# A two-layer encoder trunk: the memory's keys and values become the first chunk of work, and the start is laid out anew around them

## The chip, the cores and the metric

The kernel runs on one core of a Trainium2 chip. The metric is the device time of one execution in microseconds; where it is run several times, the median counts.

## What is computed

A trunk of two layers over 512 tokens of width 1024, with 256 memory tokens beside it. Layer 0 mixes tokens by dilated window attention with three windows, layer 1 by grouped-query attention; both also attend to the memory with four heads. Cut to what matters:

```python
for i in range(DEPTH):
    h = rmsnorm(x, norm_g[i])
    mem_h = rmsnorm(mem, mem_norm_g[i])
    ...
        proj = jnp.einsum('bsd,de->bse', h, w_in_a[j])
    ...
    kv = jnp.einsum('bnd,de->bne', mem_h, w_kv).reshape(Bn, N, 2, MEM_HEADS, HEAD_DIM)
    k = rmsnorm(kv[:, :, 0], kn_g)
    v = kv[:, :, 1]
    ...
    y = jnp.concatenate([o_mix, o_mem], axis=-1) * jax.nn.silu(gate)
    x = x + jnp.einsum('bse,ed->bsd', y, w_out[i])
```

The memory's keys and values of a layer depend on `mem`, a norm row and `w_mem_kv` alone, so they can be made at any time before the memory attention of that layer.

## The kernel before, in words

Every projection is done in float32 by three matmuls in a reduced format: each operand is split into a high part (a cast on ScalarE, ACT) and a remainder (a subtraction on VectorE, DVE). `mm3` (L162) issues the three. A weight piece of 128x1024 goes through three steps: a load of 512 KB (`W.dma`, L224), the cast into `wh` (L285) and the remainder into `wo` (L295). `wh` and `wo` have four buffers each (`RING`), so the cast of a piece waits until TensorE (PE) has read the piece four places before.

The list `PLAN` names the chunks of the program. There are two kinds. `s_chunk` (L352) is one level of Strassen's scheme: seven products in place of eight, and for these VectorE or POOL's transfers also make sums of weight quarters (T1 on VectorE at L251, T2, T3 and T4 by accumulating transfers; in the very first chunk T2 too on VectorE, L259) and VectorE makes sums of the activations. `chunk` (L331), reached through `proj_t` (L485), is a plain product without sums. Before, the order at the start is: the value product of the first attention group (`s_chunk(512, H, ev_v0, pre=second)`, 14 groups of 12 matmuls), the memory's keys and values (`mem_kv(0, ...)`, L593, two chunks of four groups), then the memory queries (`s_chunk(256, H, ev_qm)`), whose matmuls are 256 columns wide.

Each engine runs its own list in order. The order is set by the order of the Python calls and by a small driver that counts groups as slots: `spawn(gen, delay)` lets a generator do a step every so many slots. `prep()` makes the rest of the normed and transposed x, `setup()` the gain products and, on POOL, the rotary tables (L878), `mem_norm(0)` loads and norms the memory.

The norm of a token block is three functions: `norm_1` (L450) makes sums of squares on ScalarE (or half on VectorE) and the inverse root on POOL, `norm_2` (L463) multiplies on VectorE by the root and by the norm row, `norm_3`/`put_h`/`turn4` (L467) transpose four 128x128 blocks on TensorE and split them on ScalarE and VectorE. The norm row is needed on all 128 partitions: `row_bank` (L557) makes it by a product with a row of ones in TensorE, which leaves it in PSUM; `row_load` (L551) loads it 128 times over, 512 KB.

Results of products lie in four PSUM banks (`pj`, L146) that are given out in turn. A bank is free when its last reader is done. The keys are read out of their bank twice: by the sums of squares on ScalarE (L529) and by `head_mul` on VectorE (L534). The values are read by L608 on ScalarE and L610 on VectorE.

Of the kernel before, what the change touches and what calls it, by code (L numbers as in the profile page):

```python
# [21 lines left out]
TCKW = {}  # L22
NBIG, NM4, NS2, SCRATCH = 7, 23, 13, 2048
RING, LEAD = 4, 2
XW, BOTH = (1, 2, 0, 5), False
BULK, ACTIVE, MEM_AT, SET_AT, WARM, MEM_B, PREP_Y, ACC_AT, PREP_B, HALF, SET_B = 2, 2, 5, 15, 1, 12, 1, 4, 1, {"a": 3, "b": 3, "o": 0}, 11
MEM_STEP = 1, 1
MEM_D = 4
PD, W_EARLY = 1, True
EO = 1, 2, 2, 1, 1  # L30
YB = {"m": (2, 2), "k": (1, 1, 1), 0: (1, 2, 1), 1: (1, 2, 1)}
Y = [3, 2, 2, 2, 3, 2, 2, 1, 1, 1]
# [1 line left out]
A_ORDER = "01234567mab"  # L34

PLAN = ["W2"] + ["T2"] * 2 + ["W1", "W2s"] + ["W2" if c.isdigit() else "W1" for c in A_ORDER[1:]] + ["W2"] + ["O1"] * 2 + ["T2b"] * 2 + ["W1b"] * 7 + ["W2b"] + ["O1"] * 2
T1_DMA = 17
KEEP = {"T2": 6, "T2b": 4, "O1": 4, "W1": 9, "W2": 10, "W2s": 9, "W1b": 7, "W2b": 9}


class Driver:
# [83 lines left out]
def trunk_kernel(ctx: ExitStack, tc: tile.TileContext, x, mem, wall, norm_g, mem_norm_g, gcol,  # L125
# [48 lines left out]
    LOADS = (("21", "21"), ("11", "11"), ("T1", "12"), ("T2", "22"), ("22", "22"), ("T3", "12"))  # L174
    GROUPS = {"T2": (2, 2), "T2b": (2, 2), "O1": (1, 4)}

    class Weights:
        def __init__(self):
            self.items, self.last, self.need, self.allocs, self.sums = [], [], [], [], []
            self.users = {}  # L180
            d = g = 0
            for c, kind in enumerate(PLAN):
                base = len(self.items)
                if kind in GROUPS:
                    units, nb = GROUPS[kind]
                    for u in range(units):
                        for x in (2 * u, 2 * u + 1):
                            self.items.append((c, "P", x))
                            self.last.append(g + (u + 1) * nb - 1)
                            self.allocs.append(((c, "P", x), d, kind))  # L190
                            self.users[c, "P", x] = 1
                            d += 1
                        self.need += [base + 2 * u + 2] * nb
                    g += units * nb
                else:
                    n = 1 if kind in ("W1", "W1b") else 2
                    at = {k: d + i * n for i, k in enumerate(("21", "11", "12", "22"))}
                    d += 4 * n
# [11 lines left out]
            assert d == wall.shape[0], (d, wall.shape)  # L210
# [27 lines left out]
        def sum(self, force=False, want=None):  # L238

            for n, (key, d) in enumerate(self.sums[:8]):  # L240
# [3 lines left out]
                if k == "T1" and c >= T1_DMA:  # L244
                    if not self.ripe(self.load_at, key, force):
                        continue
                    G.dma_start(self.tile[key], wall[d], accum_op=ALU.add)
                elif k == "T1":
                    if not (self.ripe(self.load_at, key, force) and self.ripe(self.at, (c, "11", x), force)):
                        continue  # L250
                    V.tensor_tensor(self.tile[key], self.tile[key], self.tile[c, "11", x], ALU.add)  # L251
                    self.use((c, "11", x))
                elif k == "T2":
                    if not (self.ripe(self.load_at, key, force) and self.ripe(self.at, (c, "T1", x), force, 1 if c < T1_DMA else None)):
                        continue
                    if c:
                        G.dma_start(self.tile[key], self.tile[c, "T1", x], accum_op=ALU.add)
                    else:
                        V.tensor_tensor(self.tile[key], self.tile[key], self.tile[c, "T1", x], ALU.add)  # L259
# [15 lines left out]

        def hi(self, force=False):
            i = self.n_hi
            if i >= len(self.items) or not self.ripe(self.at, self.items[i], force, 1 if self.items[i][1] == "T1" and self.items[i][0] < T1_DMA or self.items[i][:2] == (0, "T2") else None):
# [49 lines left out]

    W = Weights()

    def chunk(units, nb, group, evac):  # L331

        ps = [None] * nb
        for u in range(units):
# [3 lines left out]
            for b in range(nb):  # L338
                if u == 0:
                    ps[b] = pj()  # L340
                group(w, u, b, ps[b])
                drv.free()
                W.advance()
# [138 lines left out]

    NAT = [nat(b) for b in range(4)]

    def proj_t(act, sels, evac):  # L485
# [5 lines left out]
        chunk(2, len(sels), group, evac)  # L491

    part = {}

# [59 lines left out]
        nc.sync.dma_start(t, src.to_broadcast([128, D]))  # L554
        rows[name] = halves(t)

    def row_bank(name, times=1):  # L557

        r = [at("row") for _ in range(2)]
        for j in (1, 0):  # L560
            for _ in range(times):
                T.matmul(r[j], ones, rows[name][j][0:1, :], start=True, stop=True)
# [30 lines left out]
    def mem_kv(layer, M):  # L593
# [18 lines left out]
        proj_t(M, NAT[:2], ev_k)  # L612
        proj_t(M, NAT[:2], ev_v)
        return kt_, vt_

# [220 lines left out]
    xv = x.rearrange("(p c) d -> c p d", c=4)  # L836
    xt = [m4(name="x") for _ in range(4)]
    rows = {}
    nc.scalar.dma_start(ident, ident_d)
    row0 = m4(name="row0")[0:1, :]  # L840
    nc.sync.dma_start(row0, norm_g[0:1, :])
    rows["x0"] = halves(row0)
    for c, n in enumerate(XW):
        nc.sync.dma_start(xt[c], xv[c])
        W.dma(n)
# [3 lines left out]
    nc.sync.dma_start(mask, mask_d)  # L849
    nc.sync.dma_start(tabA, tab_a.rearrange("p (b c d) -> p b c d", b=2, c=4))  # L850
    nc.sync.dma_start(grA[:, 0:3], qn_a[0:1, :, 0:32].to_broadcast([128, 3, 32]))
    nc.sync.dma_start(grA[:, 3:6], kn_a[0:1, :, 0:32].to_broadcast([128, 3, 32]))
    H, H2 = {}, {}
    xb = [halves(t) for t in xt]
    nst = {}

    def prep():

        s1, sums = [], []
        for c in range(2):  # L860
            norm_2(xb[2 + c], nst[2 + c], first)
            s1.append(sum_h(xb[2 + c]))
            yield 1
        for c in range(2):
            sums_h(H, xb[c], xb[2 + c], c, s1[c], sums)
# [2 lines left out]

    def setup():

        V.tensor_tensor(gk, gc[:, 0:3], gc[:, 3:6], ALU.mult)
        V.tensor_scalar(gk, gk, QS, None, ALU.mult)
        V.tensor_scalar(gc[:, 6:8], gc[:, 6:8], QS, None, ALU.mult)
# [5 lines left out]
                            grA[:, None].to_broadcast([128, 4, 6, 32]), ALU.mult)  # L879
            yield 1  # L880

    first = row_bank("x0", WARM)

    def busy(n):

        T.matmul(at("busy")[:, 0:n], ones, rows["x0"][0][0:1, 0:n], start=True, stop=True)

    busy(512)
    nst[0] = norm_1(xb[0], True)
    W.hi(True)  # L890
    norm_2(xb[0], nst[0], first, (1,))

    def mid():
        busy(128)
        W.lo()
        nst[1] = norm_1(xb[1], BOTH)

    put_h(H, "12", 0, xb[0][1], mid, True)
    if W_EARLY:
        W.hi(True)  # L900
    norm_2(xb[1], nst[1], first, (1,))
    norm_2(xb[0], nst[0], first, (0,))
    norm_2(xb[1], nst[1], first, (0,))

    def second():

        put_h(H, "12", 1, xb[1][1])
        if not W_EARLY:
            W.hi(True)
        put_h(H, "11", 0, xb[0][0])  # L910
        nst[2] = norm_1(xb[2], BOTH)
        W.lo()
        put_h(H, "11", 1, xb[1][0])
        W.hi(True)
        nst[3] = norm_1(xb[3], BOTH)

    drv.spawn(prep(), PD)
    drv.spawn(setup(), SET_AT)
# [7 lines left out]
        nc.sync.dma_start(v0w[2 * i + u][:, j * 512:(j + 1) * 512], t)  # L926
        yield 1

    drv.spawn(mem_norm(0), MEM_AT)
    s_chunk(512, H, ev_v0, pre=second)  # L930
    km, vm = mem_kv(0, Ms[0])

    od = dram.tile([12, 128, S], F32, name="od", bufs=1)
    o_done = set()
# [581 lines left out]
```

## Time and profile before

| | |
|---|---|
| median of three runs | 978.88 us (977.35 to 979.84) |
| the profiled execution | 977.34 us, its span 975.5 us |
| PE, DVE, ACT, POOL busy | 97%, 81%, 69%, 35% of the span |
| granted TensorE clock | 1.00 throughout |
| first real matmul | 10.11 us |
| first matmul of the memory queries | 86.81 us |

A profile row of the timeline reads: start, duration, engine, line of the kernel, operation, what it writes and reads, shape, and in brackets how long its engine had been idle and which instruction ended that. In the table of waits the columns are: who waited for whom, sum, number of times, the longest. `pj` is a bank of a product, `wh` and `wo` are the two parts of a weight piece, `xT` is a bank of transposes, `h`, `hS` and `act` are transposed activations, `sn` is a result taken out of its bank.

### The profile page before, as it was taken

The numbers are of one execution on the slowest core, as the hardware profiler recorded it, in microseconds if no ns is written. First come the engines' busy times: TensorE is split into PE (matmuls) and PEld (weight loads), VectorE is DVE, ScalarE is ACT, GpSimd is POOL, SyncE is SP. The second block draws the span as 40 slices with busy tenths as digits, with TensorE's granted clock in tenths as the row PEclk, the third lists the DMA queues.
The fourth block names the chain that finished last, engine by engine and source line by source line (L and its number), as shares of the span: only waits on it lengthen the run. The fifth ranks groups of instructions, "written<-read, shape, count | busy, mean of one in ns | idle before, by whom it ended". The sixth has DMA issues, their size and how long they took to land.

```text
span 975.5 us, 16658 instructions
## 1 busy us (share of the span) xinstructions
PE 949.6 (97%) x5728; PEld 836.1 (86%) x5728; DVE 791.0 (81%) x1409; ACT 675.0 (69%) x1687; POOL 343.6 (35%) x484
## 2 busy tenths in 40 slices
PE   8899999999999999999999998998999999999998
PEld 5689888888888888888899996887999999998776
DVE  6997776888888888888888999768788997769863
ACT  5555689686868686868685756555588887878760
POOL 1122423556454545454635011314443231011001
PEclk9999999999999999999999999999999999999999
DMA  8979846969686868785959898879695696877644
GB/s 340 312 261 339 221 103 175 291 122 265 144 262 145 262 147 260 152 257 131 282 129 275 244 202 252 255 259 350 168 215 139 177 242 167 219 194 176 180 140 130
DMA packets 88982, 209.27 MB, mean 215 GB/s; under 512 B 25281, under 2 KB 36033, under 8 KB 88898
## 3 DMA queue, kind: packets, MB, share of 16 engines
q1 hardware_dynamic: 70034, 146.28, 43.4%
q0 software_dynamic: 17568, 59.78, 32.6%
q10 hardware_dynamic: 1296, 2.16, 0.6%
q8 instruction: 45, 0.74, 0.3%
q14 instruction: 39, 0.32, 0.1%
HBM read 157.79 MB, written 12.65 MB: 175 GB/s over the span
## 4 chain that ended last, share of the span: by engine, by line
PE 82%; DVE 6%; DMA 5%; ACT 3%; POOL 2%; issue 1%; SPq 0%; DVEq 0%; ACTq 0%; POOLq 0%
PE pj L163 21%; PE pj L165 21%; PE pj L164 21%; PE qT L541 2%; DMA og<-od 2%; PE sa L1043 1%; PE oo L1145 1%; DVE wo L295 1%; PE pt L1124 1%; PE sa L1039 1%; PE ptb L1348 1%; DMA odb<-o 1%; PE xT L471 1%; DMA wl<-wl 1%; DMA og<-odb 1%
## 5 line engine op out<-in xcount | busy, mean ns | idle before, releaser
L285 ACT CAST wh<-wl 128x1024 fp32r<-128x1024 f32 x255 | 270.4, 1062 | 82.4 <-PE pj L165 38.4
L295 DVE TENSOR_TENSOR wo<-wl,wh 128x1024 fp32r<-128x1024 f32 x255 | 314.2, 1237 | 11.9 <-ACT wh L285 11.4
L163 PE MATMUL pj<-wh,hS 128*128 128x512 f32 (+1 forms) x448 | 164.3, 367 | 1.8 <-DVE sn L377 1.8
L164 PE MATMUL pj<-wo,hS 128*128 128x512 f32 (+1 forms) x448 | 158.1, 353 | 2.6 <-DVE wo L295 2.4
L165 PE MATMUL pj<-wh,hS 128*128 128x512 f32 (+1 forms) x448 | 158.2, 353 | 0.0
L163 PE MATMUL pj<-wh,h 128*128 128x512 f32 (+1 forms) x336 | 123.4, 367 | 0.4 <-ACT h L157 0.4
L164 PE MATMUL pj<-wo,h 128*128 128x512 f32 (+1 forms) x336 | 118.8, 353 | 2.0 <-DVE wo L295 2.0
L165 PE MATMUL pj<-wh,h 128*128 128x512 f32 (+1 forms) x336 | 118.9, 354 | 0.0
L420 POOL TENSOR_TENSOR rstd<-mse,half 128x4 f32<-128x4 f32 (+2 forms) x98 | 101.8, 1039 | 8.2
L164 PEld LDWEIGHTS pj<-wo,hS 128*128 128x128 f32 x448 | 85.0, 190 | 13.4 <-DVE wo L295 3.5
L165 PEld LDWEIGHTS pj<-wh,hS 128*128 128x128 f32 x448 | 84.7, 189 | 12.4 <-DVE hS L160 0.3
L163 PEld LDWEIGHTS pj<-wh,hS 128*128 128x128 f32 x448 | 84.8, 189 | 11.7 <-DVE sn L377 2.0
L360 ACT COPY sn<-pj 128x512 f32<-128x512 f32 x132 | 73.8, 592 | 15.5 <-PE pj L165 11.8
L419 POOL TENSOR_SCALAR mse<-hss 128x4 f32<-128x4 f32 (+1 forms) x86 | 42.8, 498 | 115.2 <-ACT junk L529 111.3
L529 ACT ACTIVATE junk<-sn 128x128 f32<-128x128 f32 x264 | 79.2, 310 | 0.2 <-DVE sn L371 0.2
L987 POOL TENSOR_TENSOR ta<-sn,tabs 128x128 f32<-128x128 f32 (+1 forms) x64 | 36.9, 579 | 118.8 <-DVE sn L534 90.4
L164 PEld LDWEIGHTS pj<-wo,h 128*128 128x128 f32 x336 | 64.0, 190 | 9.6 <-DVE wo L295 2.3
L165 PEld LDWEIGHTS pj<-wh,h 128*128 128x128 f32 x336 | 63.7, 190 | 9.2 <-DVE h L160 0.2
L163 PEld LDWEIGHTS pj<-wh,h 128*128 128x128 f32 x336 | 63.9, 190 | 7.8 <-ACT h L157 0.7
L377 DVE TENSOR_TENSOR sn<-pj,sn 128x512 f32<-128x512 f32 x99 | 67.5, 683 | 3.3 <-PE pj L165 3.0
L269 POOL DMA_DIRECT2D wl<-wl x33 | 29.2, 886 | 111.3 <-DVE wo L295 58.9
L163 PE MATMUL pj<-hS,wh 128*128 128x256 f32 x192 | 55.9, 291 | 0.0
(229 smaller groups left out, 2465.7 us busy)
## 6 DMA issues: line engine op xcount, KB each, us to landing
wl<-in_wall_dram SPq DMA_DIRECT2D x222, 512.0 KB, 7.0
wl<-wl POOLq DMA_DIRECT2D x64, 512.0 KB, 5.9
wl<-in_wall_dram POOLq DMA_DIRECT2D x42, 512.0 KB, 8.3
acc<-sn POOLq DMA_DIRECT2D x16, 256.0 KB, 5.7
od<-o SPq DMA_DIRECT2D x12, 256.0 KB, 5.2
og<-od SPq DMA_DIRECT2D x12, 256.0 KB, 5.9
odb<-o SPq DMA_DIRECT2D x12, 256.0 KB, 3.6
og<-odb SPq DMA_DIRECT2D x12, 256.0 KB, 3.9
```

Of the source, the lines that this page charges most:

```text
L163: T.matmul(o, lh, rh, start=start, stop=False, skip_group_check=True)
L164: T.matmul(o, lh, rl, start=False, stop=False, skip_group_check=True)
L165: T.matmul(o, ll, rh, start=False, stop=stop, skip_group_check=True)
L269: G.dma_start(self.tile[key], self.tile[c, "T2", x], accum_op=ALU.add)
L285: A.copy(wh, self.tile[self.items[i]])
L295: V.tensor_tensor(wo, self.tile[key], wh.bitcast(F32), ALU.subtract)
L360: A.copy(t, b)
L377: V.tensor_tensor(t, b, t, ALU.subtract if q == "12" else ALU.add)
L419: G.tensor_scalar(e, ss, EPS, None, ALU.add)
L420: G.tensor_tensor(r, e, half[:, 0:n], ALU.pow)
L529: A.activation(jk, p[:, j * 128:(j + 1) * 128], AF.Square, scale=QS, accum_out=ss[:, j:j + 1])
L987: G.tensor_tensor(ta[:, 0:n], xn[:, 0:n, 0:32], ropeA[:, 0, b, s0:s0 + n], ALU.mult)
```

## The change

1. The first chunk is the memory's keys, the second its values, the third the value product of x (`SEQ = [1, 2, 0, ...]`; the layout of the weights in memory stays).
2. SP's queue at the start is: two norm rows, the memory's two blocks with two weight pieces between, two more pieces, then x with weights between. The loads of the mask and of the rotary tables, which followed the first eight weight pieces, are issued by `setup()` in the fifteenth slot, and its other steps follow four slots later.
3. The memory's norm row comes by `row_bank` from one row (before: a load of 512 KB). The layer's norm row comes through `row_bank` too, into two of the `pj` banks, and two copies on ScalarE take it from there to SBUF. The 512-wide `busy` matmul is left out.
4. The memory's first half-blocks are normed and transposed ahead of the first group; the others in `ahead(u, b)`, which the chunk calls right before a group. All four blocks of x are normed in `prep()`.
5. The T2 sum of the value product is made by POOL's transfer, as in the other chunks, and no more by VectorE.

Cut to its core:

```diff
-PD, W_EARLY = 1, True
+PD = 2
...
+SEQ = [1, 2, 0] + list(range(3, len(PLAN)))
 T1_DMA = 17
-KEEP = {"T2": 6, "T2b": 4, "O1": 4, "W1": 9, "W2": 10, "W2s": 9, "W1b": 7, "W2b": 9}
+KEEP = {"T2": 8, "T2b": 4, "O1": 4, "W1": 9, "W2": 10, "W2s": 9, "W1b": 7, "W2b": 9}
...
-                    if c:
-                        G.dma_start(self.tile[key], self.tile[c, "T1", x], accum_op=ALU.add)
-                    else:
-                        V.tensor_tensor(self.tile[key], self.tile[key], self.tile[c, "T1", x], ALU.add)
+                    G.dma_start(self.tile[key], self.tile[c, "T1", x], accum_op=ALU.add)
...
+                if pre:
+                    pre(u, b)
                 group(w, u, b, ps[b])
...
+    row1 = m4(name="row1")[0:1, :]
+    nc.sync.dma_start(row1, norm_g[0:1, :])
+    rows["x0"] = halves(row1)
+    for b in range(2):
+        nc.sync.dma_start(mt[b], mem[b * 128:(b + 1) * 128])
+        W.dma(1)
+    W.dma(2)
...
+    for c in range(4):
+        nc.sync.dma_start(xt[c], xv[c])
+        if c % 2:
+            W.dma(2)
...
     def setup():
 
+        nc.sync.dma_start(mask, mask_d)
+        nc.sync.dma_start(tabA, tab_a.rearrange("p (b c d) -> p b c d", b=2, c=4))
+        nc.sync.dma_start(grA[:, 0:3], qn_a[0:1, :, 0:32].to_broadcast([128, 3, 32]))
+        nc.sync.dma_start(grA[:, 3:6], kn_a[0:1, :, 0:32].to_broadcast([128, 3, 32]))
+        yield 4
...
-    first = row_bank("x0", WARM)
+    first = row_bank("m0", WARM)
+    gain = row_bank("x0", 1, pj)
+    rows["x"] = halves(m4(name="row"))
+    for j in (1, 0):
+        A.copy(rows["x"][j], gain[j])
...
-    busy(512)
-    nst[0] = norm_1(xb[0], True)
+    mb, M = [halves(t) for t in mt], Act(NM)
+    nst = [norm_1(mb[0], True)]
     W.hi(True)
-    norm_2(xb[0], nst[0], first, (1,))
+    norm_2(mb[0], nst[0], first, (0,))
...
+    def ahead(u, b):
+
+        if (u, b) == (0, 1):
+            norm_3(mb[1], M, 128, 0)
+            for c in range(2):
+                norm_2(mb[c], nst[c], first, (1,))
+        if (u, b) == (1, 0):
+            for c in range(2):
+                norm_3(mb[c], M, 128 * c, 1)
...
-    drv.spawn(mem_norm(0), MEM_AT)
-    s_chunk(512, H, ev_v0, pre=second)
-    km, vm = mem_kv(0, Ms[0])
+    km, vm = mem_kv(0, M, ahead)
+    s_chunk(512, H, ev_v0)
```

What stands in the engines' lists at two places follows. First ScalarE's list at the start, before; `x_78` and `x_79` are the first two blocks of x, `wh_130` is the first weight piece:

```order
L434 ACTIVATE warm_76<-half_72 128x1
L839 DMA ident_68<-in_ident_dram 128x128
L458 ACTIVATE sq_119,ss_118<-x_78 128x512
L285 CAST wh_130<-wl_86 128x1024
L458 ACTIVATE sq_144,ss_143<-x_79 128x512
L458 ACTIVATE sq_146,ss_143<-x_79 128x512
L157 CAST h12_134<-xT_135 128x4x128
```

The same place after; `m_82` and `m_83` are the memory's blocks, `row_119` and `row_118` the banks with the layer's norm row:

```order
L438 ACTIVATE warm_76<-half_72 128x1
L844 DMA ident_68<-in_ident_dram 128x128
L906 COPY row_122<-row_119 128x512
L906 COPY row_122<-row_118 128x512
L462 ACTIVATE sq_130,ss_129<-m_82 128x512
L287 CAST wh_141<-wl_90 128x1024
L462 ACTIVATE sq_154,ss_153<-m_83 128x512
L462 ACTIVATE sq_156,ss_153<-m_83 128x512
L158 CAST act_125<-xT_145 128x4x128
```

Two copies that read the third and fourth row products now stand ahead of the first square.

Then VectorE's list around the head norms of the memory's keys (`xn<-pj`), before; `wl_665` is a weight sum of the memory queries, and around the norms stand weight remainders only:

```order
L251 TENSOR_TENSOR wl_665<-wl_665,wl_663 128x1024
L295 TENSOR_TENSOR wo_717<-wl_562,wh_716 128x1024
L295 TENSOR_TENSOR wo_720<-wl_601,wh_719 128x1024
L295 TENSOR_TENSOR wo_760<-wl_640,wh_759 128x1024
L295 TENSOR_TENSOR wo_763<-wl_659,wh_762 128x1024
L534 TENSOR_TENSOR xn_830<-pj_673,rstd_774 128x512
L295 TENSOR_TENSOR wo_825<-wl_661,wh_824 128x1024
L295 TENSOR_TENSOR wo_828<-wl_663,wh_827 128x1024
L534 TENSOR_TENSOR xn_848<-pj_700,rstd_807 128x512
```

The same norms after; `x_78` to `x_81` are the blocks of x, `xs` and `hS` the sums of them and their transposed form, `wo_435` and `wo_438` the first two weight remainders of the value product:

```order
L469 SCALAR_TENSOR_TENSOR x_81<-x_81,rstd_385,row_122 128x512 x2
L510 TENSOR_TENSOR xs1_442<-x_81 128x512
L538 TENSOR_TENSOR xn_444<-pj_177,rstd_353 128x512
L297 TENSOR_TENSOR wo_435<-wl_190,wh_434 128x1024
L297 TENSOR_TENSOR wo_438<-wl_192,wh_437 128x1024
L161 TENSOR_TENSOR hS1_463<-xT_464,hS1_463 128x4x128
L518 TENSOR_TENSOR xs2_461<-xs1_391,x_78 128x512
L519 TENSOR_TENSOR x_80<-x_78,x_80 128x512
L520 TENSOR_TENSOR xs4_462<-x_78,xs2_461 128x512
L538 TENSOR_TENSOR xn_474<-pj_198,rstd_416 128x512
```

The norms of the keys now stand among the preparation of x. `pj_177` and `pj_198` are the first two product banks given out after the norm row's two; the value product's first two banks, `pj_514` and `pj_515`, come four banks later.

More of the change, by code (lines that the diff above doesn't have):

```diff
@@ L24 @@
 RING, LEAD = 4, 2
-XW, BOTH = (1, 2, 0, 5), False
-BULK, ACTIVE, MEM_AT, SET_AT, WARM, MEM_B, PREP_Y, ACC_AT, PREP_B, HALF, SET_B = 2, 2, 5, 15, 1, 12, 1, 4, 1, {"a": 3, "b": 3, "o": 0}, 11
+BULK, ACTIVE, SET_AT, WARM, MEM_B, PREP_Y, ACC_AT, PREP_B, HALF, SET_B = 2, 2, 15, 1, 12, 1, 4, 1, {"a": 3, "b": 3, "o": 0}, 11
 MEM_STEP = 1, 1
 MEM_D = 4
-PD, W_EARLY = 1, True
+PD = 2
 EO = 1, 2, 2, 1, 1
@@ L175, in trunk_kernel, with pieces @@
     GROUPS = {"T2": (2, 2), "T2b": (2, 2), "O1": (1, 4)}
+    def pieces(kind):
+        return 2 * GROUPS[kind][0] if kind in GROUPS else 4 if kind in ("W1", "W1b") else 8
     class Weights:
@@ L180, in __init__ @@
             self.users = {}
-            d = g = 0
-            for c, kind in enumerate(PLAN):
+            g = 0
+            for c in SEQ:
+                kind, d = PLAN[c], sum(pieces(k) for k in PLAN[:c])
                 base = len(self.items)
@@ L209, in __init__ @@
                             g += 1
-            assert d == wall.shape[0], (d, wall.shape)
+            assert sum(pieces(k) for k in PLAN) == wall.shape[0]
             self.g = -1
@@ L277, in hi @@
             i = self.n_hi
-            if i >= len(self.items) or not self.ripe(self.at, self.items[i], force, 1 if self.items[i][1] == "T1" and self.items[i][0] < T1_DMA or self.items[i][:2] == (0, "T2") else None):
+            if i >= len(self.items) or not self.ripe(self.at, self.items[i], force, 1 if self.items[i][1] == "T1" and self.items[i][0] < T1_DMA else None):
                 return False
@@ L329, in trunk_kernel, with chunk @@
     W = Weights()
-    def chunk(units, nb, group, evac):
+    def chunk(units, nb, group, evac, pre=None):
         ps = [None] * nb
@@ L483, in trunk_kernel, with proj_t @@
     NAT = [nat(b) for b in range(4)]
-    def proj_t(act, sels, evac):
+    def proj_t(act, sels, evac, pre=None):
         def group(w, u, b, p):
@@ L490, in group @@
                 mm3(p, sels[b](act, 0, kk), sels[b](act, 1, kk), w[k][0], w[k][1], kk == 0, kk == 7)
-        chunk(2, len(sels), group, evac)
+        chunk(2, len(sels), group, evac, pre)
     part = {}
@@ L555, in row_load, with row_bank @@
         rows[name] = halves(t)
-    def row_bank(name, times=1):
-        r = [at("row") for _ in range(2)]
+    def row_bank(name, times=1, bank=at):
+        r = [bank("row") for _ in range(2)]
         for j in (1, 0):
@@ L591, in put_norm, with mem_kv @@
         yield 1
-    def mem_kv(layer, M):
+    def mem_kv(layer, M, pre=None):
         kt_ = [m4(F32R, "kmT").rearrange("p (h t) -> p h t", h=4) for _ in range(2)]
@@ L610, in ev_v @@
             V.scalar_tensor_tensor(vt_[1][:, b], p, 0.5, vt_[0][:, b].bitcast(F32), ALU.mult, ALU.subtract)
-        proj_t(M, NAT[:2], ev_k)
+        proj_t(M, NAT[:2], ev_k, pre)
         proj_t(M, NAT[:2], ev_v)
@@ L838, in trunk_kernel @@
     rows = {}
+    mt = [m4(name="m") for _ in range(2)]
     nc.scalar.dma_start(ident, ident_d)
     row0 = m4(name="row0")[0:1, :]
[L841 to L845, printed above, removed]
+    nc.sync.dma_start(row0, mem_norm_g[0:1, :])
+    rows["m0"] = halves(row0)
+    row1 = m4(name="row1")[0:1, :]
[5 more added lines that the diff above has]
+    W.dma(2)
     tabA = s2(name="tabA")[:, 0:256].rearrange("p (b c d) -> p b c d", b=2, c=4)
@@ L848, in trunk_kernel @@
     nc.sync.dma_start(gc, gcol)
[L849 to L852, printed above, removed]
+    for c in range(4):
+        nc.sync.dma_start(xt[c], xv[c])
+        if c % 2:
+            W.dma(2)
     H, H2 = {}, {}
     xb = [halves(t) for t in xt]
-    nst = {}
     def prep():
[L859 to L862, printed above, removed]
+        s1, sums, n = [], [], {}
+        for c in range(5):
+            if c < 4:
+                n[c] = norm_1(xb[c])
+            if c:
+                norm_2(xb[c - 1], n[c - 1], rows["x"])
+                if c > 2:
+                    s1.append(sum_h(xb[c - 1]))
+            if 1 < c < 4:
+                put_h(H, "12", c - 2, xb[c - 2][1])
+                put_h(H, "11", c - 2, xb[c - 2][0])
             yield 1
@@ L880, in setup @@
             yield 1
-    first = row_bank("x0", WARM)
+    first = row_bank("m0", WARM)
[3 more added lines that the diff above has]
+        A.copy(rows["x"][j], gain[j])
     def busy(n):
-        T.matmul(at("busy")[:, 0:n], ones, rows["x0"][0][0:1, 0:n], start=True, stop=True)
-    busy(512)
-    nst[0] = norm_1(xb[0], True)
+        T.matmul(at("busy")[:, 0:n], ones, rows["m0"][0][0:1, 0:n], start=True, stop=True)
+    mb, M = [halves(t) for t in mt], Act(NM)
+    nst = [norm_1(mb[0], True)]
     W.hi(True)
-    norm_2(xb[0], nst[0], first, (1,))
+    norm_2(mb[0], nst[0], first, (0,))
     def mid():
@@ L895, in mid @@
         W.lo()
[L896 to L915, printed above, removed]
+        nst.append(norm_1(mb[1]))
+    turn4(mb[0][0], M.block(0, 0, slice(0, 128)), M.block(1, 0, slice(0, 128)), mid)
+    W.hi(True)
+    norm_2(mb[1], nst[1], first, (0,))
+    W.lo()
+    def ahead(u, b):
[6 more added lines that the diff above has]
+                norm_3(mb[c], M, 128 * c, 1)
     drv.spawn(prep(), PD)
```

1 line of the change is left out of this document (removed).

## The prediction

> **What bounds the kernel now.** I read the page first, then the table of stretches over the first 90 us, then the waits of the first 60 us, then the timeline there. TensorE has little to give away over the whole program:
>
> ```profile
> PE 949.6 (97%) x5728; PEld 836.1 (86%) x5728; DVE 791.0 (81%) x1409; ACT 675.0 (69%) x1687; POOL 343.6 (35%) x484
> ```
>
> It is idle for 975.5 − 949.6 = 25.9 us, so a change that leaves the matmuls as they are can only win or lose in the stalls. The stretches show where they are (columns: length, busy time and count of PE, PEld, DVE, ACT, POOL, granted clock, DMA share, GB/s):
>
> ```profile
> 0.00:10.11 10.11, 7.29 (x13) 3.04 (x13) 2.90 (x7) 5.12 (x11) 1.54 (x9) 1.00 0.79 292
> 10.11:15.70 5.59, 4.78 (x18) 3.82 (x19) 3.89 (x6) 2.66 (x6) 0.63 (x2) 1.00 1.02 416
> 15.70:22.60 6.90, 6.90 (x33) 5.67 (x32) 6.63 (x9) 5.52 (x13) 2.35 (x6) 1.00 0.89 327
> 22.60:39.45 16.85, 12.26 (x63) 9.24 (x61) 16.82 (x23) 7.78 (x11) 3.70 (x4) 1.00 1.04 301
> 39.45:90.00 50.55, 50.55 (x254) 42.76 (x255) 42.22 (x49) 30.78 (x59) 11.28 (x15) 1.00 0.89 300
> ```
>
> The first real matmul starts at 10.11; from 22.6 to 39.45 VectorE is busy for 16.82 of 16.85 us and TensorE waits for it; from 39.45 TensorE is never idle in this table. So the change is decided by when the real work starts and by what VectorE still owes TensorE.
>
> ```profile
> PE pj L164 <- DVE wo L295: 4.4, 3, 2.0
> ```
>
> **The point of comparison.** Both programs do the same three things first (the value product of layer 0 and the memory's keys and values) and then come to the 256-wide matmuls of the memory queries. Before:
>
> ```profile
> 16.25 0.39 PE L165 MATMUL pj<-wh,h 128*128 128x512 f32 x1
> 16.48 0.39 PE L163 MATMUL pj<-wh,h 128*128 128x512 f32 x1
> 86.45 0.60 PE L541 MATMUL qT<-ident,xn 128*128 128x128 f32 x4
> 86.81 0.36 PE L163 MATMUL pj<-wh,h 128*128 128x256 f32 x1
> 89.75 0.60 PE L541 MATMUL qT<-ident,xn 128*128 128x128 f32 x4
> ```
>
> They start at 86.81, with one set of four transposes (89.75) still to come; a set holds TensorE for about 0.44 us (the one at 86.45 is less than 0.36 ahead of the next matmul's record, and pairs of sets below take 0.8 to 0.9), so the old program is level with a new one at 87.25. A 512-wide matmul costs 0.23 (16.25 to 16.48). I now work out the same moment for the changed program. Behind it both have the same instructions in nearly the same order, so I let the difference stand to the end.
>
> **Start: the row products and ScalarE's queue.** The old start:
>
> ```profile
> 2.35 3.75 PE L562 MATMUL row<-row,ones 1*128 1x512 f32 x4 [2.35 <-DMA row<-in_norm_g_dram]
> 5.03 0.63 ACT L458 ACTIVATE sq<-x 128x512 f32<-128x512 f32 x1 [2.81 <-DMA x<-in_x_dram]
> 5.89 1.91 PE L886 MATMUL busy<-row,ones 1*128 1x512 f32 x2
> 7.09 0.75 DVE L465 SCALAR_TENSOR_TENSOR x<-x,rstd,row 128x512 f32<-128x512 f32 x1 [1.36 <-POOL rstd L420]
> 7.89 1.11 PE L471 MATMUL xT<-ident,x 128*128 128x128 f32 x4
> 9.49 0.56 ACT L157 CAST h<-xT 128x512 fp32r<-128x512 f32 x1
> 10.11 0.79 PE L163 MATMUL pj<-wh,h 128*128 128x512 f32 x1 [0.38 <-ACT h L157]
> 19.84 1.07 ACT L360 COPY sn<-pj 128x512 f32<-128x512 f32 x2
> ```
>
> A row product is two PE instructions of about 0.86 us: two products, four instructions, run from 2.35 to 6.10, and the busy one ends at 7.80. The change drops the busy one and makes four row products: the third ends at 7.8, the fourth at 7.8 + 1.7 = 9.5. ScalarE copies both new rows out before it squares the memory, in one queue: the second copy runs from 9.55 to 10.1 (0.54 each, row 19.84). The memory's own tile is third in SP's queue where x was second, which puts its landing near 5.4 by my estimate (x 5.03, issues some 0.4 apart); it is not what is waited for. From ScalarE's square to the first matmul the old rows give 7.09 − 5.03 = 2.06 (square, rstd), 0.80 (norm to transposes), 1.11 (transposes) and 0.62 (cast to matmul), with 0.05 for a semaphore: 4.6 us. **The first real matmul moves from 10.11 to 10.1 + 4.6 = 14.7.** What stands behind the two copies on ScalarE is all of its work: squares, casts of weights, casts of transposes.
>
> **First chunk.** A cold matmul costs 0.43 against 0.23 later:
>
> ```profile
> 11.98 0.63 PE L164 MATMUL pj<-wo,h 128*128 128x512 f32 x1
> 12.41 0.63 PE L165 MATMUL pj<-wh,h 128*128 128x512 f32 x1
> 12.83 1.65 PE L471 MATMUL xT<-ident,x 128*128 128x128 f32 x8
> 38.03 1.03 PE L471 MATMUL xT<-ident,xs 128*128 128x128 f32 x8
> 38.82 0.48 PE L163 MATMUL pj<-wh,hS 128*128 128x512 f32 x1
> ```
>
> It lasted some 5 us from the first matmul, so I charge the first group of 12 at 0.43: 14.7 + 5.1 = 19.8. The three groups that follow cost 12 × 0.23 = 2.73 each; three transpose sets cost 1.3 (eight in 38.03 to 38.82 took 0.8); and since they now stand right ahead of the groups that read them, TensorE waits each time for ScalarE's cast (0.62) and VectorE's remainder: about 0.95 and 0.65. The chunk ends at 19.8 + 8.2 + 1.3 + 1.6 = 30.9.
>
> TensorE's clock: the granted column is 1.00 in every stretch, and the row products from 2.35 to 7.80 left the matmuls at 11.98 cold. The Trainium skill (TensorE: Matmul & The Clock Gate, What's actually happening) says that one busy window of about 3.4 us lets the clock go to full. By that rule four unbroken row products would be fast by the last one, the start would come 0.85 us sooner, and the sum would end 0.85 lower. The old rows, cold after 5.4 us of row products, speak against it.
>
> **VectorE's debt, moved.** At 30.9 the last weight buffer of the ring is free: ScalarE casts one weight (1.0) and squares a token block (1.3) before it casts the first transposed block of x, so VectorE's part of that starts at about 34.0. From there to the head norm of the second key block VectorE has 16 instructions of 512 columns and 6 of 1024 in its queue. Their pace:
>
> ```profile
> 8.25 1.34 ACT sq L458 x4
> 27.04 0.68 DVE L514 TENSOR_TENSOR xs<-xs,x 128x512 f32<-128x512 f32 x1
> 27.64 0.69 DVE L515 TENSOR_TENSOR x<-x 128x512 f32<-128x512 f32 x1
> 22.12 1.40 DVE L465 SCALAR_TENSOR_TENSOR x<-x,rstd,row 128x512 f32<-128x512 f32 x2
> 28.84 1.22 DVE L295 TENSOR_TENSOR wo<-wl,wh 128x1024 fp32r<-128x1024 f32 x1
> 29.98 1.22 DVE L259 TENSOR_TENSOR wl<-wl 128x1024 f32<-128x1024 f32 x1
> ```
>
> 12 × 0.60 + 4 × 0.70 (the norms) + 6 × 1.14 = 16.8, so the head norm ends at 50.9. It reads the bank `pj_198`; the banks go round in fours, and the value product's second, `pj_515`, is that same one: **TensorE can't begin it before 51.0.** Unhindered it would be there at 46: 30.9, plus 4 groups (10.9), five transpose sets (2.2) and six matmuls (1.4) is 45.4, plus a wait or so. Five us go there. Before, the keys and values were projected from 64.7 on, behind the value product, and no value product stood behind their banks:
>
> ```profile
> L163 PE MATMUL pj<-wh,act x32: 389/389/389, 64.7 to 85.8; 128*128 128x512 f32 x32
> tabs<-in_mask_dram SPq DMA_DIRECT2D x1, 256.0 KB, 8.2
> ```
>
> From 51.0 the value product has 168 − 6 = 162 matmuls, 36.9 us; nine transpose sets, 4.0; and one more wait of about 0.8 for the bank of the first value block of the memory, which VectorE splits late for the same reason. **That is 92.6, against 87.25: 5.4 us later.**
>
> **Parts that cost nothing here.** The mask and table loads leave the start of SP's queue and go behind the first store of the value product. The tables are read by POOL's table products (66.80 in the old program), which now run four groups later, and by nobody before them. VectorE's small gain products stand behind the landing of these loads; the mask, the largest, took 8.2 us, and the driver leaves four groups, 4 × 2.73 = 10.9. Were that cover gone, the weight remainders queued behind the gain products would wait, and TensorE for them. POOL's two products cost VectorE something:
>
> ```profile
> 66.80 1.84 POOL L878 TENSOR_TENSOR tabs<-tabA,grA 128x768 f32<-128x768 f32 x1 [12.56 <-DVE grA L875]
> 67.23 2.48 DVE L295 TENSOR_TENSOR wo<-wl,wh 128x1024 fp32r<-128x1024 f32 x1
> 70.78 4.53 DVE L295 TENSOR_TENSOR wo<-wl,wh 128x1024 fp32r<-128x1024 f32 x2
> wl<-wl POOLq DMA_DIRECT2D x64, 512.0 KB, 5.9
> ```
>
> A remainder under them takes 2.5 to 3.4 us in place of 1.2. Before, they stood apart and the ring of four weights hid it; now they are back to back, and I take it as hidden again, with 0 to 3.3 us as the bound. The adds that the old first chunk did on VectorE (L259, 1.14 twice) become transfers of 5.9 us on POOL; they are issued near 39, as soon as VectorE's sums are made, and first read by the seventh group of the value product, some 15 us behind 51.0. The mem row's broadcast load of 512 KB is gone; no TensorE wait hung on it.
>
> **Sum.** The profiled execution took 977.34 with a span of 975.5. Plus 5.4 it is 982.7; the median of the runs, 978.88, is 1.5 higher, so I forecast 978.9 + 5.4 = **984.3 us**. The unknowns: the row products' clock (−0.9 to 0), the cold stretch (−1 to +1), VectorE's pace (±1), the tables (0 to +3.3).
>
> **The rivals.** *No debt.* If VectorE keeps up, the new order starts late but never stalls: 30.9 + chunk two's 10.9 + 38.2 + 16 transpose sets (7.0) is 87.0, level with 87.25: 978.7. For it: the new first chunks need no sums of weights, and VectorE has 22 us more of TensorE work to hide x's norms behind. Against it: the queue is counted above, and 16.8 us stand between 34.0 and a bank that is wanted at 46. It decides if VectorE's part can start 5 us sooner.
>
> *Faster.* If the copies did not hold ScalarE (row products at the warm pace would end near 6), the start would be about 11 and, with no debt, the sum 83.4: 975.0. It needs both; the second row of ScalarE's queue speaks against it.
>
> *Slower still.* The tables' two products hit the remainders at the end of the value product, where TensorE follows closely: up to 3.3 more, 987.6.
>
> **How the numbers follow.** About 0.3%, 2.9 us, is what a measurement of this kernel can tell from no change. My forecast gets 0.70 (982 to 986), no debt 0.14, faster 0.05, slower still 0.11. Faster by over 0.3% is then 0.05; the no-debt case and a sliver of the forecast give 0.15 for the same; 0.80 for slower. The range leaves out the faster case, most of no debt and the end of slower still: 980.3 to 987.5.
>
> **What would show it.** In the profile after: the first 512-wide matmul near 14.7, its cast behind two copies of rows on ScalarE; VectorE without a gap from 34 to about 60; a TensorE wait of 3 us or so at 48 to 51 at the second bank of the value product; the first 256-wide matmul near 92.6. I am wrong if the start is under 12, or if that matmul comes before 90, or if the difference at 95 us is not the difference at the end.

## The result, and the profile after

The changed kernel takes 984.06 us (median of 13 runs, 980.95 to 988.51), the kernel before 977.35 (13 runs, 975.57 to 981.38). The ratio is 1.0064, with a 95% interval of 1.0049 to 1.0080: slower by about 6.3 us. (One run of e1 below, 1908.96 us, and one of the kernel before beside it, 4413.87 us, are in a slow state and count in no ratio.)

The profiled execution took 985.6 us with a span of 983.7, 8.2 more than the span of before. The busy times of the changed kernel, and the granted clock in 40 equal slices of the span, have this to set beside the old ones:

```profile
PE 955.7 (97%) x5730; PEld 840.0 (85%) x5730; DVE 787.5 (80%) x1407; ACT 676.3 (69%) x1689; POOL 346.7 (35%) x486
...
PEclk9989999999999999999999999999999999999999
```

TensorE is busy for 6.1 us more, though it has only two instructions more in 5730. The row products account for 1.5 us of it (7.16 us below, against 3.75 and 1.91 before). And one of the clock's slices, the third, is no longer at the top: some matmuls ran longer. The start, from the timeline:

```profile
2.31 7.16 PE L566 MATMUL row<-row,ones 1*128 1x512 f32 x8 [2.31 <-DMA row<-in_mem_norm_g_dram]
...
7.80 0.59 ACT L906 COPY row<-row 128x512 f32<-128x512 f32 x1 [5.58 <-PE row L566]
...
9.50 0.59 ACT L906 COPY row<-row 128x512 f32<-128x512 f32 x1 [1.12 <-PE row L566]
...
9.99 0.63 ACT L462 ACTIVATE sq<-m 128x512 f32<-128x512 f32 x1
...
12.80 1.12 PE L475 MATMUL xT<-ident,m 128*128 128x128 f32 x4 [3.33 <-DVE m L469]
...
14.59 0.79 PE L164 MATMUL pj<-wh,act 128*128 128x512 f32 x1
...
19.45 0.45 PE L166 MATMUL pj<-wh,act 128*128 128x512 f32 x1
```

The eight instructions of the row products end at 9.47, the second copy follows at 9.50, ScalarE squares the memory only behind it at 9.99, and the first real matmul runs at 14.59. The stretch where the keys end and the value product begins:

```profile
45.30 0.68 DVE L538 TENSOR_TENSOR xn<-pj,rstd 128x512 f32<-128x512 f32 x1
...
48.21 0.40 PE L166 MATMUL pj<-wh,h 128*128 128x512 f32 x1
...
49.97 0.68 DVE L520 TENSOR_TENSOR xs<-x,xs 128x512 f32<-128x512 f32 x1
...
50.57 0.68 DVE L538 TENSOR_TENSOR xn<-pj,rstd 128x512 f32<-128x512 f32 x1
...
51.31 0.80 PE L164 MATMUL pj<-wh,h 128*128 128x512 f32 x1 [2.71 <-DVE xn L538]
...
51.90 0.63 PE L165 MATMUL pj<-wo,h 128*128 128x512 f32 x1
...
52.33 0.63 PE L166 MATMUL pj<-wh,h 128*128 128x512 f32 x1
...
54.04 1.91 PE L475 MATMUL xT<-ident,xs 128*128 128x128 f32 x8
...
56.45 0.78 PE L164 MATMUL pj<-wh,h 128*128 128x512 f32 x1
...
57.30 0.39 PE L166 MATMUL pj<-wh,h 128*128 128x512 f32 x1
...
95.05 0.28 PE L164 MATMUL pj<-wh,h 128*128 128x256 f32 x1
```

TensorE waits 2.71 us for the head norm that frees the bank. And then the matmuls run at 0.43 apiece (52.33 is 0.43 behind 51.90, and the record is 0.63 long where it is 0.39 later). The stretches of this place say why (length, busy time of PE, PEld, DVE, ACT, POOL, granted clock, DMA share, GB/s):

```profile
49.00:51.00 2.00, 0.00 (x0) 0.00 (x0) 2.00 (x4) 0.00 (x0) 0.00 (x0) 0.82 1.01 254
51.00:53.00 2.00, 1.69 (x4) 1.40 (x5) 2.00 (x5) 0.00 (x0) 0.00 (x0) 0.50 1.03 334
53.00:55.00 2.00, 2.00 (x8) 1.60 (x8) 2.00 (x4) 0.00 (x0) 1.01 (x2) 0.50 1.09 281
55.00:57.00 2.00, 2.00 (x10) 1.93 (x9) 2.00 (x3) 1.60 (x4) 1.67 (x2) 0.50 1.08 227
57.00:59.00 2.00, 2.00 (x10) 1.63 (x9) 2.00 (x4) 1.58 (x3) 0.00 (x0) 0.97 1.07 205
50.00:50.50 0.50, 0.00 (x0) 0.00 (x0) 0.50 (x2) 0.00 (x0) 0.00 (x0) 0.78 1.02 262
57.00:57.50 0.50, 0.50 (x3) 0.42 (x2) 0.50 (x2) 0.50 (x2) 0.00 (x0) 0.89 1.08 213
```

The granted clock was half from 50.28 (0.78 in the half microsecond from 50.0) to 57.11 (0.89 in the one from 57.0), 6.8 us. In the profiled execution of before it was 1.00 in every stretch. Six matmuls and three sets of transposes took 5.1 us, from 51.31 to 56.45, where they cost 1.4 + 1.3 = 2.7 at the full clock; TensorE was busy throughout.

The granted clock says nothing of the slow matmuls at the start, in this kernel or in the one before: the trace's record of it begins 30.72 us ahead of the fall, at 19.56, and the 1.00 that the stretches ahead of that show is no reading.

The times of the changed kernel go with the mean granted clock of each run:

| mean granted clock | times, us |
|---|---|
| 0.999 | 980.95 |
| 0.998 | 981.37, 981.63, 982.36 |
| 0.997 | 981.07 |
| 0.995 | 983.75, 984.06, 984.53 |
| 0.994 | 985.41, 985.60, 986.71 |
| 0.993 | 986.37, 988.51 |

About 1.1 us for each 0.001, by a straight line through the thirteen. A mean clock lower by 0.001 is 0.98 us of clock missing in 983, so what the clock loses shows in the time, since TensorE is what the time goes by. It does not explain everything: in the two sets of runs of the kernel before that stand beside the experiments the line is flatter, about 0.7, and one of their runs took 976.66 us with a mean clock of 0.948.

### The profile page after: what moved, and what is told of

It reads as the page before. It is cut to its first block, busy times and chain, and to the rows that moved or that the text cites. A ratio compares the mean times of both kernels' runs of the same rounds, so it can differ in the third digit from the quotient of the medians.

```text
span 983.7 us, 16684 instructions
## 1 busy us (share of the span) xinstructions
PE 955.7 (97%) x5730; PEld 840.0 (85%) x5730; DVE 787.5 (80%) x1407; ACT 676.3 (69%) x1689; POOL 346.7 (35%) x486
## 5 line engine op out<-in xcount | busy, mean ns | idle before, releaser
L424 POOL TENSOR_TENSOR rstd<-mse,half 128x4 f32<-128x4 f32 (+2 forms) x98 | 99.7, 1018 | 8.2
L538 DVE TENSOR_TENSOR sn<-sn,rstd 128x512 f32<-128x512 f32 (+1 forms) x82 | 47.6, 590 | 10.3 <-POOL rstd L424 10.3
```

The source lines that it names most:

```text
L424: G.tensor_tensor(r, e, half[:, 0:n], ALU.pow)
L538: V.tensor_tensor(xn[:, 0:n], p.rearrange("p (a b) -> p a b", a=4)[:, 0:n], r[:, 0:n, None].to_broadcast([128, n, 128]), ALU.mult)
```

## The experiments

My theory: the change costs in two places that are separate. ScalarE's two copies, which wait for the row products, hold the start by 3 to 5 us; and VectorE's preparation of x, no longer spread beside the value product, stands between the keys' banks and the value product, some 5 us of waits. After the result a third came: the wait lets the clock drop. Rivals: the bank alone is at fault (its reader is queued too late), not the amount of VectorE's work; the moved loads, or transfers in general, set the pace; the clock's drop is only seen and costs nothing. All times are medians, all ratios are against the kernel before in runs beside the experiment (median 977.28 for e1, e2, e3 and e5, 978.11 for the others). "Below the changed kernel" is counted from its 984.06. By the ratios the same differences are 2.7 us for e1, 4.0 for e5, 1.4 for e3, 3.4 for e6 and 7.1 for e8. The intervals of e5, e6 and e8 lie clear of the changed kernel's, those of e1 and e3 overlap it.

**The copies later (e1).**

```diff
-    for j in (1, 0):
-        A.copy(rows["x"][j], gain[j])
...
     turn4(mb[0][0], M.block(0, 0, slice(0, 128)), M.block(1, 0, slice(0, 128)), mid)
     W.hi(True)
+    for j in (1, 0):
+        A.copy(rows["x"][j], gain[j])
```

> The two copies of the layer's norm row stand behind the first casts on ScalarE, the rest is as in the changed kernel. If ScalarE's queue sets the start: the square runs near 5.2, the transposes wait only for the four row products (9.5), the first real matmul moves from 14.6 to about 11.3, everything behind it comes 3.3 us sooner, and the wait at the value product's second bank stays as long as it was, near 48. Time 3.3 us below the changed kernel, about 0.3% over the kernel before. If the moment of 51 is set by something that does not hang on the start (transfers), the start moves and the first 256-wide matmul stays near 95.

980.40 us, ratio 1.0036 (1.0017 to 1.0054): 3.7 below the changed kernel. The timeline of this kernel has the square in the place where the copies stood, and the copies behind ScalarE's first casts:

```profile
5.00 0.63 ACT L462 ACTIVATE sq<-m 128x512 f32<-128x512 f32 x1 [2.78 <-DMA m<-in_mem_dram]
...
11.27 0.79 PE L164 MATMUL pj<-wh,act 128*128 128x512 f32 x1
...
12.06 1.08 ACT L923 COPY row<-row 128x512 f32<-128x512 f32 x2
...
47.70 0.51 PE L164 MATMUL pj<-wh,h 128*128 128x512 f32 x1 [2.69 <-DVE xn L538]
...
89.44 0.28 PE L164 MATMUL pj<-wh,h 128*128 128x256 f32 x1
```

The start moved by 3.32, the bank's moment by 3.61, with a wait of the same length. In this profile the clock stayed at 1.00 behind that wait; other runs of the same kernel have a lower mean clock (0.993 to 0.999, 983.27 to 978.00 us), where in the run is not on record. The queue is a cause of its own, and the moment of 51 hangs on the start.

**The row by a load (e5, and e7 for a second trace).** It undoes this part of the change: no row products for x's norm row, no copies.

```diff
-    row1 = m4(name="row1")[0:1, :]
-    nc.sync.dma_start(row1, norm_g[0:1, :])
-    rows["x0"] = halves(row1)
...
     W.dma(2)
+    row_load("x", norm_g[0:1, :])
...
-    gain = row_bank("x0", 1, pj)
-    rows["x"] = halves(m4(name="row"))
-    for j in (1, 0):
-        A.copy(rows["x"][j], gain[j])
```

> The layer's norm row comes by a broadcast load of 512 KB behind the first weights, with no row products and no copies; all else as in the changed kernel. If the row through TensorE and its copies cost the start: first matmul near 10, 4.5 us sooner, first 256-wide matmul near 90, time about 4.5 us below the changed kernel and within 0.3% of the kernel before, the wait at the second bank still there. If the added load of 512 KB matters (1.3 us of all transfer engines ahead of x), the norm of x comes later and half of that is lost again.

978.71 us, ratio 1.0023 (1.0008 to 1.0038): 5.4 below the changed kernel. Its first matmul and the bank:

```profile
9.64 0.80 PE L164 MATMUL pj<-wh,act 128*128 128x512 f32 x1 [0.25 <-ACT act L158]
...
46.58 0.79 PE L164 MATMUL pj<-wh,h 128*128 128x512 f32 x1 [2.72 <-DVE xn L538]
```

The start is 4.95 us sooner, the bank 4.7, and the wait is there again. The added load of 512 KB, which stands ahead of x, took at most 0.2 us back. The kernel's second trace:

> The kernel with the norm row loaded by broadcast once more, for its trace beside the others of this chip: first matmul near 9.6, the wait of 2.7 us at the second bank and, if the idle window falls that way, a granted clock under 1.00 behind it.

978.12 us in one run, with a mean clock of 0.996: the first matmul at 9.22, a wait of 2.72 us at the bank (46.49), and a clock at half around it, for half as long as in e5's trace.

**The head norm earlier (e2).**

```diff
             r = head_sq(p)
-            yield 2
+            yield 2 - (layer == 0)
             xn = head_mul(p, r)
```

> The head norm of the memory's keys in layer 0 is made one slot earlier (first wait of ev_k 1 in place of 2), so VectorE frees the banks of the keys before the sums of x. Theory of the bank: the wait of 2.7 us at the second bank goes, and with it the cold stretch, 2.7 to 5 us below the changed kernel. Theory of the debt: VectorE has the same instructions to do before the same matmuls, so the wait goes from the bank to the next transposes of the sums of x, some 2.4 us near 52, and the time stays within 1 us of the changed kernel.

984.37 us, ratio 1.0081 (1.0063 to 1.0098): as slow as the changed kernel, with the first 256-wide matmul at 94.88 against 95.05. The wait at the bank is gone, and this is what came in its place, in the table of TensorE's waits:

```profile
PE xT L475 <- DVE xs L518: 3.7, 2, 2.3
...
PE pj L164 <- ACT sn L364: 1.2, 1, 1.2
...
PE qT L545 <- DVE xn L538: 1.1, 1, 1.1
```

The 2.3 us are at 53.20, at the transposes of the second sum of x, and the clock fell to half behind them. The theory of the bank falls: the bank is only where the debt is collected.

**Filled (e3).** Ten matmuls whose result nobody reads, ahead of the value product's second bank.

```diff
+    def fill():
+        p, w = at("busy"), W.op[W.taken - 1][0]
+        for _ in range(10):
+            T.matmul(p, H["12"][:, 0, 0, 0:128], w[:, 0:512], start=True, stop=True)
+
-    s_chunk(512, H, ev_v0)
+    s_chunk(512, H, ev_v0, pre=fill)
```

> Ten matmuls of 512 columns on data at hand stand in the wait ahead of the value product's second bank (their result is read by nobody). The bank comes free when it did, near 51.3, so a theory of waits alone expects no change. If the idle time lets the clock drop, the granted clock stays at 1.00 from 49 to 57, the six matmuls and three sets of transposes behind it run at full pace, the first 256-wide matmul comes near 92.7 in place of 95.05, and the time is up to 2.4 us lower, with less scatter between runs.

981.22 us, ratio 1.0050 (1.0032 to 1.0068), 2.8 below the changed kernel, and six runs within 979.90 to 983.93, with a mean clock of 0.998 or 1.000 in each. The bank came free when it did, half a microsecond later even, but the first 256-wide matmul is 1.4 sooner:

```profile
51.85 0.50 PE L164 MATMUL pj<-wh,h 128*128 128x512 f32 x1 [0.43 <-DVE xn L538]
...
54.57 0.48 PE L164 MATMUL pj<-wh,h 128*128 128x512 f32 x1
...
93.61 0.28 PE L164 MATMUL pj<-wh,h 128*128 128x256 f32 x1
```

Its stretches, with columns as above:

```profile
50.00:57.00 7.00, 6.57 (x36) 5.26 (x35) 7.00 (x10) 3.02 (x5) 2.42 (x3) 1.00 1.05 280
```

What took 5.1 us in the changed kernel takes 2.7 here (51.85 to 54.57). In the time alone this is not clear of noise (1.4 us by the ratios). But no run of the six has a mean clock under 0.998, where eight of the changed kernel's thirteen have 0.995 or less: that speaks for the idle TensorE as what lets the clock fall.

**Sums by transfer (e6).** VectorE is rid of two sums of 1.14 us in the queue ahead of the bank.

```diff
-                if k == "T1" and c >= T1_DMA:
+                if k == "T1" and (c >= T1_DMA or c == 0):
                     if not self.ripe(self.load_at, key, force):
                         continue
                     G.dma_start(self.tile[key], wall[d], accum_op=ALU.add)
```

> The two T1 sums of the value product's weights (1.14 us each on VectorE, in the queue ahead of the bank) are made by POOL's accumulating transfers from memory; all else as in the changed kernel. Theory of the debt: VectorE is 2.3 us earlier at the head norm, the second bank comes free at 49 in place of 51.3, and the time falls by 2.3 us, or by more where the shorter wait no longer lets the clock drop. If transfers were short there, the casts of these sums wait and nothing is won.

981.33 us, ratio 1.0029 (1.0013 to 1.0045), 2.7 below the changed kernel. The bank came free at 48.41, and what the clock did behind a wait of 2.24 us is the remarkable part:

```profile
45.79 0.39 PE L166 MATMUL pj<-wh,h 128*128 128x512 f32 x1
...
48.41 0.55 PE L164 MATMUL pj<-wh,h 128*128 128x512 f32 x1 [2.24 <-DVE xn L538]
```

Its stretches, with columns as above:

```profile
48.00:50.00 2.00, 1.59 (x4) 1.29 (x5) 2.00 (x4) 0.00 (x0) 0.00 (x0) 0.68 1.08 252
50.00:52.00 2.00, 2.00 (x9) 1.66 (x8) 2.00 (x4) 0.01 (x1) 0.12 (x1) 0.50 0.98 250
52.00:54.00 2.00, 2.00 (x14) 1.77 (x13) 2.00 (x3) 2.00 (x4) 0.75 (x1) 0.97 1.07 266
```

Two sums less, 2.9 us sooner at the bank. Of these 0.7 are there ahead of the sums: VectorE's first split of x starts at 33.59 against 34.26, because the slow matmuls of the start ended earlier in this execution (at 17.9, not 19.5). The other 2.2 are the two sums. So VectorE's debt is real, and its size is that of the instructions in the queue. The clock fell all the same, and only after TensorE was at work again (0.68 in the two microseconds from 48, that is at 48.71).

**The tables early (e4).** The four loads of mask and tables are issued at the start, and the gain products run in slot 15. The loads stand behind those of x in SP's queue, not ahead of them as the expectation has it.

```diff
+    nc.sync.dma_start(mask, mask_d)
+    nc.sync.dma_start(tabA, tab_a.rearrange("p (b c d) -> p b c d", b=2, c=4))
+    nc.sync.dma_start(grA[:, 0:3], qn_a[0:1, :, 0:32].to_broadcast([128, 3, 32]))
+    nc.sync.dma_start(grA[:, 3:6], kn_a[0:1, :, 0:32].to_broadcast([128, 3, 32]))
     H, H2 = {}, {}
...
     def setup():
 
...
-        yield 4
```

> Mask and tables are loaded at the start again, ahead of x, and the gain products follow in slot 15; all else as in the changed kernel. My forecast charged nothing for this edit: within 1 us of the changed kernel. If the loads at the start cost (0.5 MB ahead of x, 1.3 us) the norms of x come later and the debt grows by as much; if POOL's two table products under VectorE cost TensorE time where they stand now, it is up to 3.3 us faster.

984.69 us, ratio 1.0075 (1.0052 to 1.0098): the changed kernel's time. Three of its runs have a mean clock of 0.996 to 1.000 and 982.13 to 982.64 us, three have 0.993 or 0.994 and 986.73 to 987.66 us. Its bank came free 1.0 us sooner, at 50.31, but VectorE's first split was 1.0 us sooner already, for the reason given under e6. So this edit costs nothing and brings nothing that can be seen, and the rival of the moved loads falls with it. A load ahead of x is in e5, where it cost nothing either.

**All three (e8).** The load of e5, the sums of e6, and six filling matmuls in the way of e3.

> The norm row by a broadcast load, the two T1 sums by transfers, and six filling matmuls ahead of the second bank. If the three costs are separate they add: 4.5 to 5 us for the start, 2.3 for the debt, up to 2.4 for the clock, 8 to 10 us below the changed kernel, that is 1 to 3 us below the kernel before. If what follows waits for transfers, part of it is given back behind the memory queries and the time equals that of the kernel before.

977.22 us, ratio 0.9991 (0.9976 to 1.0006): 6.8 below the changed kernel, and not to be told from the kernel before. At the first 256-wide matmul the expected 8 to 10 us were there:

```profile
9.21 0.79 PE L164 MATMUL pj<-wh,act 128*128 128x512 f32 x1
...
84.72 0.28 PE L164 MATMUL pj<-wh,h 128*128 128x256 f32 x1
```

95.05 − 84.72 is 10.3 us. Of these, 3.0 were given back behind it (span 976.4 against 983.7, a gain of 7.3). The stretches of this execution show where the clock was low:

```profile
600.00:620.00 20.00, 20.00 (x100) 17.12 (x99) 15.04 (x20) 10.26 (x15) 1.73 (x2) 0.92 0.56 162
700.00:750.00 50.00, 47.75 (x388) 47.55 (x388) 40.26 (x58) 35.64 (x98) 19.46 (x23) 0.97 0.74 159
940.00:960.00 20.00, 18.17 (x72) 14.34 (x71) 11.53 (x15) 5.34 (x7) 3.49 (x4) 0.91 0.64 157
```

20 × 0.08 + 50 × 0.03 + 20 × 0.09 = 4.9 us of clock missing, against 20 × 0.09 = 1.8 in the same three stretches of the changed kernel's profile (0.91, 1.00, 1.00). The difference, 3.1, is about what was given back. Waits of 1 to 2.6 us stand ahead of these places in the kernel before and in the changed one too; in which run they bring the clock down differs (the twelve runs of e8 have mean clocks from 0.994, 978.52 to 979.32 us, to 0.999, 974.01 us; the slowest, 980.75, has 0.996). I expected 1 to 3 us below the kernel before and measured 0.9, with an interval from 2.3 below to 0.6 above.

**What the low clock costs.** The nine traces of the changed kernel and its variants settle it. The second bank's first matmul and the first 256-wide one have the same TensorE work between them in each but e2, and the clock was at half, around the bank and later, in whole steps of 3.41 us:

| trace | clock at half near the bank, us | from the bank to the first 256-wide matmul, us | clock at half behind that, us | from there to the end, us |
|---|---|---|---|---|
| e1 | 0 | 41.74 | 0 | 886.7 |
| e3 | 0 | 41.76 | 0 | 885.3 |
| e8 | 0 | 41.75 | 3 x 3.41 | 891.7 |
| e6 | 3.41 | 42.64 | 0 | 885.0 |
| e4 | 3.41 | 42.66 | 3.41 | 887.4 |
| e7 | 3.41 | 42.38 | 3.41 | 887.5 |
| e2 | 3.41 | not comparable | 3.41 | 887.5 |
| changed | 6.83 | 43.74 | 3.41 | 888.6 |
| e5 | 6.83 | 43.83 | 3.41 | 886.3 |

One step near the bank costs 0.6 to 0.9 us, two cost 2.0 to 2.1; behind it, those with none took 885.0 to 886.7, those with one 886.3 to 888.6, and the one with three 891.7. So the rival that the clock's drop costs nothing falls. It also shows that filling one wait is not enough: the steps behind it remain a matter of the run.

## Why the prediction was right, point by point

- **The start.** Forecast 14.7, measured 14.59; the reason, ScalarE's copies behind the row products, is shown by e1 (3.3 us of start, 3.7 of time) and e5 (4.95 and 5.4). By the ratios the times are 2.7 and 4.0. The row products did not get faster on the way: by the copies behind them (7.80 and 9.50) the fourth still took 1.7 us. So the 0.85 us that the prediction weighed against its sum did not come.
- **First chunk.** Forecast end 30.9; the transposes behind it began at 31.28. The cold stretch lasted from 14.59 to 19.45, 4.9 us, forecast 5.
- **VectorE's debt.** Forecast 34.0 for its first split, 50.9 for the head norm's end, 51.0 for the second bank. Measured:

```profile
34.26 1.29 DVE L161 TENSOR_TENSOR h<-xT,h 128x512 fp32r<-128x512 f32 x2 [1.53 <-ACT h L158]
...
35.47 2.35 DVE L297 TENSOR_TENSOR wo<-wl,wh 128x1024 fp32r<-128x1024 f32 x2
```

  and 51.31 for the bank. That it is the amount of work and not the bank's place is shown by e2 and e6.
- **What was missing.** The forecast went on from 51.0 with 36.9 + 4.0 + 0.8 to 92.6 (the terms add up to 92.7); it was 95.05. The bank accounts for 0.3 of the difference. The step that failed is the pace behind it: six matmuls and three transpose sets ran at half the clock, which the sum did not have. Its 41.7 us from the bank on are what the traces with the clock at full show (41.74 to 41.76); the changed kernel took 43.74. I weighed the clock at the start only and took it for settled after that. The 0.8 for the bank of the first value block never came in the changed kernel, since TensorE was late enough; in e3, where it was not, it is there (`vm L614`, 0.6).
- **The total.** Forecast 5.4 more, measured 6.7 by the medians and 8.2 by the two profiled spans. Whether 5.4 is right for a run whose clock holds is not settled. The changed kernel's run at 0.999 took 980.95: 3.6 above the profiled run of before, 977.34 at 1.00, but 4.6 to 6.2 above the other four runs of before at 0.999 or 1.000 (974.73 to 976.32). That my forecast of 984.3 lies by the median of 984.06 is partly luck: the median of the kernel before, on which I put the 5.4, came out 1.5 lower over thirteen runs, and the lower clock, which I did not have, made up for it. Nor does the difference at the first 256-wide matmul simply stand to the end, as I let it: it did in this pair of traces (95.05 against 87.25, 7.8, then 8.2), but in e3 6.4 us there became 3.4 at the end.
- **The parts at no cost.** The tables are settled by e4. POOL's table products did what was feared (two remainders under them took 5.29 us in place of 2.35), and no wait of TensorE followed, so "slower still" falls too. What fillers would cost elsewhere stays open: no kernel here has every wait filled.
- **The rivals.** "No debt" falls by the wait of 2.71 us, and by e2 and e6; "faster" needed both causes away, and e8, which takes both down, was 2.5 us ahead at the first 256-wide matmul (84.72 against 87.25) and still only drew level at the end.

The Trainium skill (TensorE: Matmul & The Clock Gate, What's actually happening) has the gate decide on free-running windows of about 3.4 us, and lets it close after an idle window. The length of the low stretch agrees: 6.8 us are two such windows, and the 3.41 of e2, e4, e6 and e7 are one. That it closed with waits of 2.71 and 2.24 us, shorter than a window, is not what that sentence leads one to expect; the measurement decides.

## What to carry to other kernels

When work is moved to the front, read each engine's queue for what it stands before: two copies of 0.6 us cost 3.3 us of the start because they waited for TensorE ahead of ScalarE's first useful instruction. Sum an engine's whole queue up to the instruction that is waited for; moving that instruction up only moves the wait. And price a wait of TensorE by what comes behind it as well: a wait of 2 to 3 us cost up to 2 us more at half the clock here, and with matmuls that nobody reads in that wait (e3) the clock stayed up.

## What the runs showed of the hardware

- The granted clock fell to half with a wait of 2.71 us (changed kernel, 50.28 to 57.11, the fall within the wait) and one of 2.24 us (e6, 0.3 us after the next matmul had begun), and stayed at 1.00 behind one of 2.69 us (e1's profile). So whether a wait of this length brings the clock down differs from run to run.
- Between two changes the trace's record of the clock always holds a whole number of steps of 3.41 us: low for 3.41 or 6.83, high for 30.72 (changed kernel) or 34.13 (e2, e4) before the fall, nine and ten steps. In the one step before the fall near the bank TensorE was idle for 1.9 us (changed kernel) to 2.3 (e7). That e1's wait was split over two steps would explain why its clock held, but is not shown.
- Row products with one row of ones, 7.2 us without a break, left the matmuls that followed 5 us later at the slow pace: 0.43 apiece from 14.59 to 19.45. A wait of 3.33 us stands between, but in the kernel before, where the row products run to 7.80 and no wait is over 0.4 us, the matmuls from 10.11 on took 0.43 too.
- A weight remainder of 1.22 us on VectorE took 2.6 us on average while POOL made the rotary tables:

```profile
85.44 4.64 POOL L898 TENSOR_TENSOR tabs<-tabA,grA 128x768 f32<-128x768 f32 x2 [2.13 <-DVE grA L895]
...
85.87 5.29 DVE L297 TENSOR_TENSOR wo<-wl,wh 128x1024 fp32r<-128x1024 f32 x2
```
